# Hybrid encoder layer on Trainium2: where the FFN's first blocks take their weights, and in which order they multiply

## The chip, the cores and the metric

The program runs on one core of one Trainium2 chip. Its engines are TensorE (PE, matrix products), VectorE (DVE), ScalarE (ACT), GpSimd (POOL), and SyncE (SP), which here only issues DMAs. The metric is the device time of one execution in microseconds; the kernel before stands at the median of 3 runs. Where the trace is quoted, times are microseconds from the start of the profiled execution's span, and L12 is line 12 of the kernel that ran.

## The reference, cut to what matters

A layer has three sub-layers with residual adds: token mixing (a gated delta rule beside a spatial gating branch), cross-attention into 256 memory tokens, and a dense SwiGLU FFN. It is computed for two inputs with shared weights: a prompt of 1024 tokens and a sample of 256, D_MODEL 1024, D_FF 2816, all in float32. The change lies where the second sub-layer ends and the third begins:

```python
def rmsnorm(x, w):
    xf = x.astype(jnp.float32)
    y = xf * lax.rsqrt(jnp.mean(xf * xf, -1, keepdims=True) + EPS)
    return (y * w.astype(jnp.float32)).astype(x.dtype)

def encoder_layer(x, mem, ...):
    ...
    x = x + memory_cross_attention(rmsnorm(x, norm_xa_w), rmsnorm(mem, norm_mem_w), xa_w_q, xa_w_kv, xa_w_o)
    h = rmsnorm(x, norm_ffn_w)
    gu = h @ ffn_w_gate_up
    x = x + (jax.nn.silu(gu[..., :D_FF]) * gu[..., D_FF:]) @ ffn_w_down
    return x
```

## The kernel before, in words

Tokens lie in three blocks (b): prompt tokens 0 to 511 (b=0), 512 to 1023 (b=1) and the sample (b=2, 256 columns). A tile x0, x1 or x2 holds one block, features on partitions, in 8 pieces k of 128 features.

A product in float32 precision is three passes: each operand is split into hi (a rounded copy that ACT makes) and lo (the rest, a subtraction on DVE or POOL). `split` (L126 and the line above it) does this; `mm3` issues hi·hi, lo·hi and hi·lo for each 128-row piece, all on line L108. So a "product" below of a 512-column block with 4 pieces is 12 matmuls.

`OutProj.run` (L1227) makes the last projection of the attention, block by block, product m by product m, adds it to x (`evac`, L1237) and collects the squares for the norm: ACT squares (nsq, L248), DVE adds (nacc, L249). `Norm.rest` finishes a norm as a side stream: four or two small matmuls sum nacc over partitions, DVE makes the rsqrt in eleven small operations (L224 to L228, the result is nst), more small matmuls spread nst over the partitions ("the nst matmuls"), DVE scales x (L284) and the pieces are split. Side streams are fed between the matmuls of the main stream by a counted clock of planned matmul time; LAGS and LAGS2 (L2047) are the planned delays in the sample's norm, ahead of the summing matmuls and of the nst matmuls.

The FFN's way up is written with combined operands, which save products: with the two halves of the prompt and of the features, the sinks make differences of the normalised blocks (r1 into block 1's h tiles, L1427; r2 in PSUM banks, L1431; t3, L1538; t4, L1547), each split into hi and lo, and POOL makes sums of gate and up weights. For each f of 22 pieces of D_FF there are four weight pairs: gu_w[f,0] is the gate, [f,1] and [f,2] are sums (`gu_sa`, `gu_sb`), [f,3] is up. w(i) below is gu_w[f,i].

`ff_first` issues f=0 for the prompt and the first two products of f=1 (pn, pn2); `ff_up(1)` starts with the sample's f=0 and f=1 (sg0, su0, sg, su), which need the sample's norm to be done, and ends with f=1's rest; f≥2 is one steady pattern. PE runs matmuls in the order in which the code issues them: before, from the end of the projection, b21·w(0), b11·w(0), r1·w(1), r2·w(1), b22·w(2), then pn, pn2 with gu_w[1,0], then t3·w(2), t4·w(3), the nst matmuls, sg0, su0, sg, and f=1's r2, r1, t3, su, t4, b22. The order on the other engines is a scheduler's, from the code's data flow and estimated times. A queue runs its operations in order.

Before the change, the splits of w(2), w(3) of f=0 and of the gate of f=1 are on DVE (the lines of `split(..., V)` and `gu_gate(1, V)`), and f=1's raw weights are loaded inside ff_first (L1724, L1741). r2 and t3 have tiles of their own in a pool "comb"; sums are made in a tile "room" that is taken when x0 is free.

Of the kernel before, what the change touches and what calls it, by code (L numbers as in the profile page):

```python
# [17 lines left out]
P = 128  # L18
# [145 lines left out]
def trunk_kernel(ctx: ExitStack, tc: tile.TileContext, a):  # L164
# [1040 lines left out]
    class OutProj:  # L1205
# [18 lines left out]
            for m, b in FIRST_PS:  # L1224
                yield from self.parts(m, b, range(KT - 2))

        def run(self, xsrc, scale, wcol, xpool, store, sinks=None, then=None, ready=None):  # L1227

            ps = (xpool,) * 3 if sinks is None else (x0p, xhp, xpool)
            x = [p.tile([P, KT, n], F32, tag=f"x{b}", name=f"x{b}") for b, (p, (_, n)) in enumerate(zip(ps, BLOCKS))]  # L1230
            for ks in (slice(0, 2), slice(2, 8)):
                for b, (t0, n) in enumerate(BLOCKS):
                    SY.dma_start(x[b][:, ks, :], xsrc[:, ks, t0 : t0 + n])
            nms = [Norm(xpool, n) for _, n in BLOCKS]

            def evac(m, b, ps):
                V.scalar_tensor_tensor(out=x[b][:, m, :], in0=ps, scalar=scale, in1=x[b][:, m, :], op0=ALU.mult, op1=ALU.add)  # L1237
# [230 lines left out]
    def gu_sa(f):  # L1468
# [7 lines left out]
        G.tensor_tensor(out=s[:, :512], in0=s[:, 512:], in1=g[:, :512], op=ALU.add)  # L1476
# [15 lines left out]

    def first_weights():
# [23 lines left out]
    ts = ExitStack()  # L1517
    tpool = ts.enter_context(pool("comb"))
# [5 lines left out]
    r2, t3 = ([tpool.tile([P, 4, 512], F32R, tag=f"{name}{i}", name=f"{name}{i}") for i in "hl"] for name in ("r2", "t3"))  # L1524
    gu_w[0, 2], gu_w[0, 3] = pair_of(tpool), pair_of(tpool)

    def parts(hl, k, src, eng):
        split(hl[0][:, k, :], hl[1][:, k, :], src, eng)

    for k in range(4):  # L1530
        parts(r2, k, r2_raw[k], V)
    split(*gu_w[0, 2], gu_raw[0][0], V)
    fs = ExitStack()
    t4 = []

# [6 lines left out]
    def make_t4():  # L1542
        nonlocal fp
        fp = fs.enter_context(pool("ffn", side="right"))
        t4.extend(fp.tile([P, 4, 512], F32R, tag=f"t4{i}", name=f"t4{i}") for i in "hl")
        for k in range(4):
# [3 lines left out]
    def make_room():  # L1550
        nonlocal room
        room = x0p.tile([P, KT, 512], F32, tag="x0", name="room")

    fp = room = None

    turns = {"s": 0, "p": 0}

    def sum_room():
# [8 lines left out]
        S.activation(t, ps, AF.Copy)  # L1567
        return t

    def gu_mm(ps, w, i, x, start):  # L1570

        yield from mm3(ps, [(*wk(w, 4 * i + k), x[0][:, k, :], x[1][:, k, :]) for k in range(4)], start, True, not start)
# [144 lines left out]
    def ff_first():  # L1717
# [6 lines left out]
        SY.dma_start(raw, a["w_gu"][1])  # L1724
# [12 lines left out]
        t2 = gate_of(pf, u2)  # L1737
        make_t4()
        split(*gu_w[0, 3], gu_raw[0][1], V)
        raw = K.raw()[:, :1024]  # L1740
        SY.dma_start(raw, a["w_gu"][NFF + 1])  # L1741
        gu_raw[1].append(raw)
        make_room()
# [6 lines left out]
        c22 = copied(pa, second_block(0))  # L1750
        V.tensor_tensor(out=c22, in0=c22, in1=pe, op=ALU.add)
        times_up(t2, c22, store2(0), -1.0, c22)
        yield from gu_mm(pa, w(3), 1, t4, False)
        times_up(t1, pa, store1(0), -1.0)
        pending["last"] = 0, t1, c22

    def ff_up(f):
        w = lambda i: gu_w[f, i]
        second, last = f == 1, f == NFF - 1
        sums = lambda: (bank()[:, :NS], bank()[:, :NS])  # L1760
        if second:
            pa, pb = first_out
            p1 = copied(pa)
            t1 = gate_of(pb, p1)
            combine(*pending["last"])
            K.finish(K.pending.pop((id(h3), 2)))
            smp.extend(half(h3[2], i) for i in range(2))
            sg0, su0 = sums()
            yield from sample(sg0, gu_w[0, 0], (0, 1))
            gu_sa(1)  # L1770
            ts0 = silu2(sg0, NS)
            sg, su = sums()
            yield from sample(su0, gu_w[0, 3], (0, 1))
            times_up(ts0, su0, gsd[0], 1.0)
        else:
            pa, pb = bank(pm), bank(pm)
            yield from gu_mm(pa, w(0), 0, b11, True)
            p1 = copied(pa)
            sg, su = sums()
            yield from sample(sg, w(0), (0,))  # L1780
            yield from gu_mm(pb, w(0), 1, b21, True)
            t1 = gate_of(pb, p1)
            combine(*pending["last"])
        gu_sb(f)
        gu_load(f + 1, wp if f % 2 == 0 else x2p)
        yield from sample(sg, w(0), (0, 1) if second else (1,))
        yield from gu_mm(pa, w(1), 0, r2, False)
        u2 = copied(pa)
        gu_up(f)
# [341 lines left out]
```

## Time and profile before

| | us |
|---|---|
| runs (3) | 2257.84, 2257.11, 2254.49 |
| median | 2257.11 |
| profiled execution | 2255.0 |
| its span, first to last instruction | 2253.2 |
| mean granted TensorE clock | 0.993 |

The page counts busy time by engine over the span; the windows do so for a stretch, with the granted clock of TensorE (1.00 is full speed). A row of a timeline has start, duration, engine, line, operation, output<-inputs, and in brackets the idle time before it and who ended it. An operand named bank is in PSUM, all others here are in SBUF. In the waits, each row is a waiting engine and line, the operation it waited for, the total, the count and the longest. The touched stage is 1380 to 1464 of the span; f=2 starts at 1464.

### The profile page before, as it was taken

Reading aid. Unit: us, or ns where it says so; the run is one execution under the profiler, and the core shown is the slowest. Engines: PE = TensorE matmul, PEld = TensorE weight load, DVE = VectorE, ACT = ScalarE, POOL = GpSimd, SP = SyncE. Lnnn points to the kernel's source line nnn. Section 1 sums busy time; section 2 is a strip of 40 time slices with the busy share of each in tenths; the row PEclk is TensorE's granted clock in tenths of the full one; section 3 lists DMA queues with packets and bytes.
Section 4 is the critical chain, followed back from the end, with each engine's and each line's share of the span. In section 5 each row is a group of like instructions: output and inputs, shape, how many; then the busy total and the mean of one; then the engine's idle time right before and its main releaser. Section 6 shows DMA issues by size and latency. Waiting matters only on the chain.

```text
span 2253.2 us, 32407 instructions
## 1 busy us (share of the span) xinstructions
PE 2196.2 (97%) x12468; PEld 1918.3 (85%) x12468; DVE 1394.0 (62%) x2770; ACT 815.5 (36%) x1481; POOL 532.7 (24%) x355
## 2 busy tenths in 40 slices
PE   6999999999999999999999999899999999999998
PEld 6988888888888898888888888688888888888888
DVE  7768788887985964664534537544334334568575
ACT  5434243433424433233343423323232323243453
POOL 3010000000000000013231331565666566300031
PEclk9999999999999999999999999999999999999999
DMA  5221322223234445962231431223222222493531
GB/s 185 83 79 68 104 69 87 77 69 95 73 111 125 159 140 165 305 236 94 84 106 45 157 143 57 75 76 110 87 82 76 88 76 82 136 363 126 198 111 57
DMA packets 191301, 262.47 MB, mean 116 GB/s; under 512 B 72410, under 2 KB 102698, under 8 KB 191146
## 3 DMA queue, kind: packets, MB, share of 16 engines
q1 hardware_dynamic: 171306, 231.30, 30.9%
q10 hardware_dynamic: 19840, 29.11, 3.5%
q8 instruction: 97, 1.59, 0.3%
q14 instruction: 58, 0.48, 0.1%
HBM read 182.19 MB, written 78.16 MB: 116 GB/s over the span
## 4 chain that ended last, share of the span: by engine, by line
PE 82%; DVE 8%; issue 4%; DMA 2%; ACT 2%; POOL 1%; SPq 0%; POOLq 0%; ACTq 0%; DVEq 0%
PE bank L108 81%; PE bank L121 1%; DMA tbd<-stage 1%; DVE acc L599 1%; DVE wlo L126 1%; DMA t<-sgd 1%; DVE nt L284 1%; DVE U L845 0%; DVE sw L903 0%; DVE lo L126 0%; DMA stage<-gtd 0%; DVE W L745 0%; DVE nacc L249 0%; DVE aT L714 0%; DVE zt L837 0%
## 5 line engine op out<-in xcount | busy, mean ns | idle before, releaser
L108 PE MATMUL bank<-hi,whi 128*128 128x512 f32 (+1 forms) x2144 | 763.3, 356 | 2.8 <-ACT whi L125 1.7
L108 PE MATMUL bank<-lo,whi 128*128 128x512 f32 (+1 forms) x2144 | 748.8, 349 | 1.1 <-POOL lo L126 1.1
L108 PE MATMUL bank<-hi,wlo 128*128 128x512 f32 (+1 forms) x2144 | 748.3, 349 | 0.9 <-DVE wlo L126 0.9
L108 PEld LDWEIGHTS bank<-hi,wlo 128*128 128x128 f32 x2144 | 406.0, 189 | 54.9 <-DVE wlo L126 1.3
L108 PEld LDWEIGHTS bank<-hi,whi 128*128 128x128 f32 x2144 | 406.9, 190 | 52.7 <-ACT whi L125 2.2
L108 PEld LDWEIGHTS bank<-lo,whi 128*128 128x128 f32 x2144 | 407.1, 190 | 49.8 <-POOL lo L126 1.4
L126 POOL TENSOR_TENSOR wlo<-raw,whi 128x1024 fp32r<-128x1024 f32 x70 | 177.8, 2542 | 377.2 <-ACT whi L125 377.2
L125 ACT ACTIVATE whi<-raw 128x1024 fp32r<-128x1024 f32 (+1 forms) x141 | 144.5, 1026 | 195.3 <-PE bank L108 146.9
L126 POOL TENSOR_TENSOR wlo<-room,whi 128x1024 fp32r<-128x1024 f32 x42 | 100.6, 2396 | 115.7 <-ACT whi L125 115.7
L108 PE MATMUL bank<-bhl,whi 128*128 128x512 f32 x408 | 125.7, 389 | 0.0
L126 DVE TENSOR_TENSOR wlo<-raw,whi 128x1024 fp32r<-128x1024 f32 (+1 forms) x71 | 82.3, 1159 | 43.6 <-ACT whi L125 41.5
L125 ACT ACTIVATE whi<-room 128x1024 fp32r<-128x1024 f32 x42 | 44.6, 1061 | 142.5 <-PE bank L108 138.6
L1796 DVE TENSOR_TENSOR room<-room,bank 128x512 f32<-128x512 f32 x21 | 14.5, 688 | 131.8 <-ACT room L1567 131.8
L108 PEld LDWEIGHTS bank<-bhl,whi 128*128 128x128 f32 x408 | 76.5, 188 | 15.9
L599 DVE SCALAR_TENSOR_TENSOR acc<-craw,sm,acc 128x510 f32<-128x510 f32 (+1 forms) x96 | 73.6, 766 | 20.5 <-ACT acc L597 19.0
L108 PE MATMUL bank<-bhl,wlo 128*128 128x512 f32 x204 | 79.5, 390 | 1.2 <-DVE wlo L126 1.2
L745 DVE TENSOR_TENSOR W<-W,UT 128x2 f32<-128x2 f32 (+30 forms) x155 | 73.2, 472 | 10.1 <-DMA W<-in_eye 5.8
L248 ACT ACTIVATE nsq<-x 128x512 f32<-128x512 f32 (+1 forms) x70 | 40.2, 583 | 102.7 <-DVE x L1237 92.4
L962 ACT ACTIVATE gs<-bank 128x512 f32<-128x512 f32 (+1 forms) x60 | 31.2, 520 | 125.2 <-PE bank L108 119.9
L1589 DVE SCALAR_TENSOR_TENSOR t<-bank,t 128x512 f32<-128x512 f32 (+1 forms) x44 | 24.6, 558 | 82.2 <-PE bank L108 82.2
L249 DVE TENSOR_TENSOR nacc<-nacc,nsq 128x512 f32<-128x512 f32 (+1 forms) x72 | 54.4, 755 | 33.2 <-ACT nsq L248 31.9
L108 PE MATMUL bank<-bhl,ahl 128*128 128x512 f32 x312 | 73.8, 392 | 0.0
(345 smaller groups left out, 4223.1 us busy)
## 6 DMA issues: line engine op xcount, KB each, us to landing
raw<-in_w_gu SPq DMA_DIRECT2D x44, 512.0 KB, 3.9
braw<-gq SPq DMA_DIRECT2D x14, 1024.0 KB, 5.4
raw<-in_w_g SPq DMA_DIRECT2D x20, 512.0 KB, 3.3
gq<-t SPq DMA_DIRECT2D x33, 256.0 KB, 2.0
gtd<-gs ACTq DMA_DIRECT2D x32, 256.0 KB, 2.0
w<-in_w_dn SPq DMA_DIRECT2D x8, 1024.0 KB, 11.9
raw<-in_w_qkv SPq DMA_DIRECT2D x12, 512.0 KB, 3.6
gq<-r SPq DMA_DIRECT2D x22, 256.0 KB, 4.3
```

Of the source, the lines that this page charges most:

```text
L108: self.nc.tensor.matmul(out, l, r, start=start, stop=stop, skip_group_check=more)
L121: self.nc.tensor.transpose(out, x, ident)
L125: self.nc.scalar.activation(hi, src, AF.Copy)
L126: (eng or self.nc.vector).tensor_tensor(out=lo, in0=src, in1=f32(hi), op=ALU.subtract)
L248: S.activation(sq, x, AF.Square)
L249: (eng or V).tensor_tensor(out=self.acc, in0=self.acc, in1=sq, op=ALU.add)
L284: V.scalar_tensor_tensor(out=t, in0=xk(k), scalar=sm[:, wcol + k : wcol + k + 1], in1=pb[:, :n], op0=ALU.mult, op1=ALU.mult)
L599: V.scalar_tensor_tensor(out=dst, in0=src, scalar=wj, in1=dst, op0=ALU.mult, op1=ALU.add)
L745: V.tensor_tensor(out=t3, in0=u3[:, i:, c:].rearrange("p j c -> p c j"), in1=XL[:, 32 * i + i : 32 * i + 32].unsqueeze(1).to_broadcast([P, ...
L962: S.activation(t, ps, AF.Tanh, scale=0.5)
L1589: V.scalar_tensor_tensor(out=out, in0=u, scalar=sign, in1=t, op0=ALU.mult, op1=ALU.mult)
L1796: V.tensor_tensor(out=c22, in0=c22, in1=pe, op=ALU.add)
```

## The change

It alters four things around the end of the projection and the start of the FFN.

- Weights: w(2) and w(3) of f=0 are split by POOL, in the sample's block of the projection, after products m=2 and m=3 (a new hook `after` in `OutProj.run`), into places of the projection's weight pool (now "comb", 6 places of whi and wlo). r2 and t3 live in the other places of that pool. The same two pairs serve as gu_w[f,2] and gu_w[f,3] of all later f (in f=1, [1,1] takes the place of [0,2] and [1,2] gets a pair of wp). The gate of f=1 is split by POOL.
- Loads: f=1's raw weights are loaded after m=3.
- Sums: `room` is x0 itself, so a sum may be written once the part of x0 has been read.
- Order of products: after b22·w(2) comes t3·w(2), then pn, pn2, then t4·w(3), whose four pieces run in the order 2, 3, 0, 1; f=1's r2 and r1 products come before the sample's sg0 and su0. f=1 has a function of its own, `second_up`. LAGS is 20500 instead of 19000 and LAGS2 4000 instead of 8000: the nst matmuls now stand ahead of t4, the summing matmuls after the third matmul of pn.

The diff, cut:

```diff
@@ OutProj.run
+                    if b == 2 and after is not None:
+                        after(m)
@@ sinks
                 split(hi[:, k, :], lo[:, k, :], t, V)
+                if k == KT - 1:
+                    r2_ready()
@@ gu_sa, gu_sb, gu_up
-        hi, lo = gu_w[f, 1] = pair_of(wp)
+        hi, lo = gu_w[f, 1] = gu_w[0, 2] if f == 1 else pair_of(wp)
-        gu_w[f, 2] = pair_of(tpool)
+        gu_w[f, 2] = pair_of(wp) if f == 1 else gu_w[0, 2]
-        gu_w[f, 3] = pair_of(tpool)
+        gu_w[f, 3] = gu_w[0, 3]
@@
-    with pool("wx2", 6) as wx2:
-        K.wx = wx2
-        K.main(op.run(x1d, 1.0, S_FFN, x2p, x2d, sinks, first_weights, copies_read))
+    tpool = ts.enter_context(pool("comb", 6))
+    K.wx = tpool
+    r2, t3 = ((Two(), Two()) for _ in range(2))
+    def after(m):
+        if m == 2:
+            gu_w[0, 2] = room_of()
+            split(*gu_w[0, 2], gu_raw[0][0], G)
+        elif m == 3:
+            gu_w[0, 3] = room_of()
+            split(*gu_w[0, 3], gu_raw[0][1], G)
+            gu_load(1, wp)
+        else:
+            for x, t in zip(r2 if m < 6 else t3, room_of()):
+                x.parts.append(t.rearrange("p (k t) -> p k t", t=512))
+    K.main(op.run(x1d, 1.0, S_FFN, x2p, x2d, sinks, first_weights, copies_read, after))
-    split(*gu_w[0, 2], gu_raw[0][0], V)
+    LAST_FIRST = (2, 3, 0, 1)
+    room = x0
@@ ff_first
-        raw = K.raw()[:, :1024]
-        SY.dma_start(raw, a["w_gu"][1])
-        gu_raw[1] = [raw]
+        make_t3()
         yield from gu_mm(pa, w(1), 0, r2, False)
-        gu_gate(1, V)
-        make_t3()
+        gu_gate(1)
         yield from gu_mm(pf, w(2), 1, b22, True)
...
-        split(*gu_w[0, 3], gu_raw[0][1], V)
+        yield from gu_mm(pa, w(2), 0, t3, False)
+        gu_sa(1)
...
         yield from gu_mm(pn2, gu_w[1, 0], 1, b21, True)
-        yield from gu_mm(pa, w(2), 0, t3, False)
-        yield from gu_mm(pa, w(3), 1, t4, False)
+        yield from gu_mm(pa, w(3), 1, t4, False, LAST_FIRST)
@@ second_up (new, for f=1)
+        combine(*pending["last"])
+        yield from gu_mm(pa, w(1), 0, r2, False)
+        u2 = copied(pa)
+        yield from gu_mm(pe, w(1), 1, r1, True)
+        K.finish(K.pending.pop((id(h3), 2)))
+        yield from sample(sg0, gu_w[0, 0], (0, 1))
+        gu_sb(1)
+        yield from sample(su0, gu_w[0, 3], (0, 1))
+        gu_up(1)
+        gu_load(2, x2p)
+        yield from sample(sg, w(0), (0, 1))
+        gu_gate(2)
+        yield from gu_mm(pa, w(2), 0, t3, False)
+        yield from sample(su, w(3), (0, 1))
+        yield from gu_mm(pa, w(3), 1, t4, False)
+        yield from gu_mm(pe, w(2), 1, b22, False)
+        gu_sa(2)
@@
-LAGS, LAGS2, FIRST_W = 19000, 8000, 9000
+LAGS, LAGS2, FIRST_W = 20500, 4000, 9000
```

What this does to the engines' queues, at three places. The number ahead of a row is its place in the queue; xN at the end are rows alike.

**ACT in the sample's block of the projection** (x_12579 is the sample's x2, x_12577 block 0's, x_12578 block 1's; whi<-raw are the copies of w(2) and w(3) of f=0). Before:

```order
808 L248 ACTIVATE nsq<-x_12578 128x512 x5
809 L248 ACTIVATE nsq<-x_12579 128x256 x2
810 L125 ACTIVATE hi_12891<-x_12577 128x512 x2
811 L248 ACTIVATE nsq<-x_12579 128x256 x2
812 L125 ACTIVATE hi_12891<-x_12577 128x512 x2
813 L125 ACTIVATE hi_12891<-x_12578 128x512
814 L248 ACTIVATE nsq<-x_12579 128x256
815 L125 ACTIVATE whi<-raw 128x1024
```

and now:

```order
808 L248 ACTIVATE nsq<-x_12578 128x512 x5
809 L125 ACTIVATE whi<-raw 128x1024
810 L248 ACTIVATE nsq<-x_12579 128x256
811 L125 ACTIVATE whi<-raw 128x1024
812 L248 ACTIVATE nsq<-x_12579 128x256
813 L125 ACTIVATE hi_12891<-x_12577 128x512 x2
```

The two weight copies moved ahead of the first two squares of the sample.

**POOL from the last split of block 0 on** (lo_12890 are block 0's, lo_13580 and lo_13571 the sample's lo parts; x_12577 as an output is the room for sums). Before:

```order
81 L126 TENSOR_TENSOR lo_12890<-x_12577,hi_12889 128x512 x4
82 L1475 TENSOR_TENSOR room<-raw 128x512
83 L1485 TENSOR_TENSOR room<-raw 128x512
84 L1476 TENSOR_TENSOR room<-room,raw 128x512
85 L1486 TENSOR_TENSOR room<-room,raw 128x512
86 L126 TENSOR_TENSOR wlo<-room,whi 128x1024
87 L126 TENSOR_TENSOR lo_13580<-x_12579,hi_12893 128x256 x4
88 L126 TENSOR_TENSOR wlo<-room,whi 128x1024
89 L126 TENSOR_TENSOR wlo<-raw,whi 128x1024
```

and now:

```order
81 L126 TENSOR_TENSOR lo_12890<-x_12577,hi_12889 128x512 x4
82 L126 TENSOR_TENSOR wlo<-raw,whi 128x1024 x2
83 L1490 TENSOR_TENSOR x_12577<-raw 128x512
84 L1480 TENSOR_TENSOR x_12577<-raw 128x512
85 L1481 TENSOR_TENSOR x_12577<-x_12577,raw 128x512
86 L1491 TENSOR_TENSOR x_12577<-x_12577,raw 128x512
87 L126 TENSOR_TENSOR wlo<-raw,whi 128x1024
88 L126 TENSOR_TENSOR wlo<-x_12577,whi 128x1024
89 L126 TENSOR_TENSOR lo_13571<-x_12579,hi_12893 128x256 x4
90 L1480 TENSOR_TENSOR x_12577<-raw 128x512
91 L1481 TENSOR_TENSOR x_12577<-x_12577,raw 128x512
```

Two weight splits (rows 82) and the split of f=1's gate (87) are new on POOL, the four sums of f=1 stand between them, and the split of the sum (88) is ahead of the sample's lo parts as before; f=2's sums follow at 90.

**DVE from the split of r2 on** (r2l and, now, wlo<-bank are r2's lo parts; t3l and wlo<-x_12578 t3's). Before:

```order
1791 L126 TENSOR_TENSOR r2l<-bank,r2h 128x512 x4
1792 L126 TENSOR_TENSOR wlo<-raw,whi 128x1024
1793 L1584 TENSOR_TENSOR copies<-copies,bank 128x512
1794 L1538 TENSOR_TENSOR x_12578<-x_12578 128x512 x2
1795 L1580 SCALAR_TENSOR_TENSOR t<-t,copies 128x512
1796 L126 TENSOR_TENSOR t3l<-x_12578,t3h 128x512 x2
1797 L1538 TENSOR_TENSOR x_12578<-x_12578 128x512 x2
1798 L126 TENSOR_TENSOR wlo<-raw,whi 128x1024
1799 L126 TENSOR_TENSOR t3l<-x_12578,t3h 128x512 x2
```

and now:

```order
1791 L126 TENSOR_TENSOR wlo<-bank,whi 128x512 x4
1792 L1612 TENSOR_TENSOR copies<-copies,bank 128x512
1793 L1568 TENSOR_TENSOR x_12578<-x_12578 128x512 x3
1794 L1608 SCALAR_TENSOR_TENSOR t<-t,copies 128x512
1795 L126 TENSOR_TENSOR wlo<-x_12578,whi 128x512 x3
1796 L1568 TENSOR_TENSOR x_12578<-x_12578 128x512
1797 L1761 TENSOR_TENSOR copies<-copies,bank 128x512
1798 L1577 SCALAR_TENSOR_TENSOR x_12577<-bank,x_12577 128x512
1799 L126 TENSOR_TENSOR wlo<-x_12578,whi 128x512
```

The weight splits are gone from DVE, and three of t3's differences now stand ahead of its first split.

More of the change, by code (lines that the diff above doesn't have):

```diff
@@ L1225, in begin, with run @@
                 yield from self.parts(m, b, range(KT - 2))
-        def run(self, xsrc, scale, wcol, xpool, store, sinks=None, then=None, ready=None):
+        def run(self, xsrc, scale, wcol, xpool, store, sinks=None, then=None, ready=None, after=None):
             ps = (xpool,) * 3 if sinks is None else (x0p, xhp, xpool)
@@ L1511, in first_weights, with __init__, __getitem__, room_of @@
         K.side(sums())
-    with pool("wx2", 6) as wx2:
-        K.wx = wx2
-        K.main(op.run(x1d, 1.0, S_FFN, x2p, x2d, sinks, first_weights, copies_read))
+    class Two:
+        def __init__(self):
+            self.parts = []
+        def __getitem__(self, key):
+            return self.parts[key[1] // 2][key[0], key[1] % 2, key[2]]
+    ts = ExitStack()
+    tpool = ts.enter_context(pool("comb", 6))
+    K.wx = tpool
+    r2, t3 = ((Two(), Two()) for _ in range(2))
+    def room_of():
+        return tuple(tpool.tile([P, 1024], F32R, tag=t, name=t) for t in ("whi", "wlo"))
+    def after(m):
[9 more added lines that the diff above has]
+                x.parts.append(t.rearrange("p (k t) -> p k t", t=512))
+    def parts(hl, k, src, eng):
+        split(hl[0][:, k, :], hl[1][:, k, :], src, eng)
+    def r2_ready():
+        for k in range(4):
+            parts(r2, k, r2_raw[k], V)
+    K.main(op.run(x1d, 1.0, S_FFN, x2p, x2d, sinks, first_weights, copies_read, after))
     x0, x1 = op.x[0], op.x[1]
-    ts = ExitStack()
-    tpool = ts.enter_context(pool("comb"))
     K.finish(K.pending.pop((id(h3), 1)))
@@ L1523, in trunk_kernel @@
     first_copies = hp.tile([P, 4, 512], F32, tag="lo2", name="copies")
[L1524 to L1531, printed above, removed]
-    split(*gu_w[0, 2], gu_raw[0][0], V)
     fs = ExitStack()
@@ L1545, in make_t4 @@
         t4.extend(fp.tile([P, 4, 512], F32R, tag=f"t4{i}", name=f"t4{i}") for i in "hl")
-        for k in range(4):
+        for k in LAST_FIRST:
             V.scalar_tensor_tensor(out=x0[:, k + 4, :], in0=r2_raw[k], scalar=-1.0, in1=x0[:, k + 4, :], op0=ALU.mult, op1=ALU.subtract)
             parts(t4, k, x0[:, k + 4, :], V)
[L1550 to L1554, printed above, removed]
+    fp = None
+    LAST_FIRST = (2, 3, 0, 1)
+    room = x0
     turns = {"s": 0, "p": 0}
@@ L1568, in copied, with gu_mm @@
         return t
-    def gu_mm(ps, w, i, x, start):
-        yield from mm3(ps, [(*wk(w, 4 * i + k), x[0][:, k, :], x[1][:, k, :]) for k in range(4)], start, True, not start)
+    def gu_mm(ps, w, i, x, start, ks=range(4)):
+        yield from mm3(ps, [(*wk(w, 4 * i + k), x[0][:, k, :], x[1][:, k, :]) for k in ks], start, True, not start)
     def ff(p, tag, name, n=512, bufs=None):
@@ L1738, in ff_first @@
         make_t4()
-        split(*gu_w[0, 3], gu_raw[0][1], V)
[L1740 to L1743, printed above, removed]
+        yield from gu_mm(pa, w(2), 0, t3, False)
+        gu_sa(1)
+        c22 = copied(pa, second_block(0))
+        V.tensor_tensor(out=c22, in0=c22, in1=pe, op=ALU.add)
+        times_up(t2, c22, store2(0), -1.0, c22)
         pn = bank(pm)
@@ L1757, in ff_up @@
     def ff_up(f):
         w = lambda i: gu_w[f, i]
-        second, last = f == 1, f == NFF - 1
+        last = f == NFF - 1
         sums = lambda: (bank()[:, :NS], bank()[:, :NS])
[L1761 to L1783, printed above, removed]
+        pa, pb = bank(pm), bank(pm)
@@ L1784, in ff_up @@
+        yield from gu_mm(pa, w(0), 0, b11, True)
+        p1 = copied(pa)
+        sg, su = sums()
+        yield from sample(sg, w(0), (0,))
+        yield from gu_mm(pb, w(0), 1, b21, True)
+        t1 = gate_of(pb, p1)
+        combine(*pending["last"])
         gu_sb(f)
         gu_load(f + 1, wp if f % 2 == 0 else x2p)
-        yield from sample(sg, w(0), (0, 1) if second else (1,))
+        yield from sample(sg, w(0), (1,))
         yield from gu_mm(pa, w(1), 0, r2, False)
@@ L1816, in up @@
         yield from ff_first()
-        for f in range(1, NFF):
+        yield from second_up()
+        for f in range(2, NFF):
             yield from ff_up(f)
```

23 lines of the change are left out of this document (20 added, 3 removed).

## The prediction

> **What bounds the kernel now.** The page first, then windows of the touched stage and of what follows it (length, busy time of PE, PEld, DVE, ACT and POOL, the granted clock, the DMA's share, GB/s):
>
> ```profile
> PE 2196.2 (97%) x12468; PEld 1918.3 (85%) x12468; DVE 1394.0 (62%) x2770; ACT 815.5 (36%) x1481; POOL 532.7 (24%) x355
> ```
>
> ```profile
> 1390.00:1400.00 10.00, 10.00 (x76) 9.59 (x75) 10.00 (x21) 6.27 (x12) 0.00 (x0) 1.00 0.00 0
> 1400.00:1410.00 10.00, 9.21 (x41) 7.25 (x41) 9.07 (x15) 4.17 (x9) 0.00 (x0) 1.00 0.32 107
> 1410.00:1420.00 10.00, 6.77 (x30) 4.76 (x30) 10.00 (x17) 6.08 (x10) 0.00 (x0) 1.00 0.14 52
> 1420.00:1430.00 10.00, 8.19 (x35) 6.08 (x33) 8.62 (x21) 2.95 (x5) 3.21 (x3) 1.00 0.14 52
> 1430.00:1440.00 10.00, 4.76 (x19) 4.17 (x20) 8.31 (x16) 4.27 (x9) 8.16 (x7) 0.54 0.33 105
> 1470.00:1790.00 320.00, 320.00 (x1694) 276.23 (x1694) 132.03 (x143) 95.23 (x129) 198.60 (x103) 1.00 0.26 89
> ```
>
> PE is the bound nearly everywhere; between 1400 and 1440 it is not. There DVE is full (10.00, 9.07, 10.00) and POOL idle until 1427. The waits of PE between 1380 and 1464 say on whom (total, times, longest):
>
> ```profile
> PE bank L108 <- DVE nst L228: 4.3, 1, 4.3
> PE bank L108 <- ACT whi L125: 1.7, 1, 1.7
> PE bank L108 <- DVE wlo L126: 0.9, 1, 0.9
> ```
>
> The longest is for nst, the rsqrt of the sample's norm, which DVE finishes late; PE's timeline around it, and the start of f=2 (its first hi,whi):
>
> ```profile
> 1428.48 0.40 PE L108 MATMUL bank<-t4h,wlo 128*128 128x512 f32 x1
> 1433.16 1.22 PE L108 MATMUL bank<-cst,nst 128*128 128x128 f32 x4 [4.28 <-DVE nst L228]
> 1435.40 0.58 PE L108 MATMUL bank<-hi,whi 128*128 128x256 f32 x1 [1.02 <-ACT hi L125]
> 1437.05 0.58 PE L108 MATMUL bank<-lo,whi 128*128 128x256 f32 x1 [1.06 <-POOL lo L126]
> 1463.82 0.39 PE L108 MATMUL bank<-hi,wlo 128*128 128x512 f32 x1
> 1464.04 0.39 PE L108 MATMUL bank<-hi,whi 128*128 128x512 f32 x1
> ```
>
> From 1470 to 1790 PE is busy for all of 320 us at full clock, and the change leaves the order of products from f=2 on alone, so it is worth what it moves 1464.04 by. The part after nst adds up: from 1433.16 to 1464.04 are 30.9 us. In them lie 60 matmuls of 512 columns at 0.227 us (1463.82 to 1464.04, the mean of neighbours), 13.6 us; 96 of 256 columns at 0.12, 11.5; the four nst matmuls, some 0.4; together 25.5. The other 5.4 are the two waits for hi and lo (start to start some 1.8 and 1.5) and some 2 us of half clock.
>
> **The lock that the change walks into.** Before, POOL does nothing while DVE is full. Where both run, DVE's operations on two SBUF operands end only after POOL's (POOL's and DVE's timelines):
>
> ```profile
> 1317.73 2.40 POOL L126 TENSOR_TENSOR wlo<-raw,whi 128x1024 fp32r<-128x1024 f32 x1 [0.31 <-ACT whi L125]
> 1318.20 2.48 DVE L249 TENSOR_TENSOR nacc<-nacc,nsq 128x512 f32<-128x512 f32 x1 [0.94 <-ACT nsq L248]
> 1379.73 0.69 DVE L249 TENSOR_TENSOR nacc<-nacc,nsq 128x512 f32<-128x512 f32 x1 [0.76 <-ACT nsq L248]
> 1429.56 1.25 POOL L1476 TENSOR_TENSOR room<-room,raw 128x512 f32<-128x512 f32 x1
> 1429.59 1.78 DVE L1580 SCALAR_TENSOR_TENSOR t<-t,room 128x512 f32<-128x512 f32 x1
> 1462.49 2.40 POOL L126 TENSOR_TENSOR wlo<-room,whi 128x1024 fp32r<-128x1024 f32 x1 [1.72 <-ACT whi L125]
> 1464.24 0.69 DVE L1584 TENSOR_TENSOR room<-room,bank 128x512 f32<-128x512 f32 x1 [2.05 <-PE bank L108]
> ```
>
> nacc takes 0.69 alone and 2.48 beside a split: it ends at 1320.68, 0.55 after POOL. So does L1580 (1431.37 against 1430.81). L1584, with one operand in a bank (PSUM), keeps its 0.69. So I charge a DVE operation on two SBUF tiles that starts while POOL runs with the rest of POOL's operation (for 256 columns ending 0.3 after it). The Trainium skill, page "SBUF — State Buffer", section "SBUF: two separate sides", speaks against the change in the same sense: the port pair of DVE and GpSimd is an exclusive lock for a whole instruction, and a DVE instruction with two SBUF inputs contends for it. By that rule the sum is the same as by the rows, which agree.
>
> **Part by part.** (1) *Splits of w(2) and w(3) go to POOL, and to products m=2 and m=3 of the sample block.* The whi copy can start when PE has read the weights whose place it takes, which is when that product is evacuated:
>
> ```profile
> 1382.45 0.42 DVE L1237 SCALAR_TENSOR_TENSOR x<-bank,x 128x256 f32<-128x256 f32 x1
> 1382.96 0.42 ACT L248 ACTIVATE nsq<-x 128x256 f32<-128x256 f32 x1 [3.26 <-DVE nst L228]
> 1384.34 0.16 DVE L228 SCALAR_TENSOR_TENSOR nst<-bank,nst 128x4 f32<-128x4 f32 x1
> 1387.18 0.43 DVE L249 TENSOR_TENSOR nacc<-nacc,nsq 128x256 f32<-128x256 f32 x1 [0.54 <-ACT nsq L248]
> 1387.52 1.40 DVE L284 SCALAR_TENSOR_TENSOR x<-x,sm,bank 128x512 f32<-128x512 f32 x2
> 1398.78 1.05 ACT L125 ACTIVATE whi<-raw 128x1024 fp32r<-128x1024 f32 x1
> 1406.15 2.48 DVE L126 TENSOR_TENSOR r2l<-bank,r2h 128x512 fp32r<-128x512 f32 x4
> 1406.89 0.50 PE L108 MATMUL bank<-r2l,whi 128*128 128x512 f32 x1 [0.79 <-DVE r2l L126]
> 1408.54 1.22 DVE L126 TENSOR_TENSOR wlo<-raw,whi 128x1024 fp32r<-128x1024 f32 x1
> ```
>
> ACT copies whi at 1382.3 to 1383.35 (1.05, L125); POOL splits 1383.4 to 1385.8 (2.40). ACT's queue now holds nsq behind that whi, so nacc comes at about 1383.7, always inside POOL's operation: it ends near 1386.05. The last links of block 1's rsqrt stand behind it; three at 0.2 us each give nst at 1386.6, not 1384.5, and PE, which has no other work queued before nst, loses **1.9 us**. m=3 repeats it: PE 1.9 late, whi 1388.0, POOL 1389.1 to 1391.5, nacc held until 1391.7, and L284 and all of block 1's normalisation behind it begin at 1391.7 instead of 1387.5: DVE is **4.2 us late**. It is full from there (windows), so the one gap of 0.9 that it had, against one more nacc held by a POOL sum of f=1 near 1402 (1.2), leaves r2l 4.2 late: 1410.35. PE is only 1.9 late when it asks, and idles some **3.3 us** before r2l, at 1411.1.
>
> (2) *DVE from r2l to nst.* In the change's order 29 operations of 512 columns stand in that stretch: 29 by 0.60 (2.48 for four, less the overlap) is 17.4; the rsqrt's 11 small ones at 0.2 are 2.2; a wait for ACT's silu, queued behind gate(1)'s whi, 0.6. Three DVE splits of 1.22 are gone. Three operations meet POOL: t3's first difference a sum of f=1 (0.9), the two silu products the splits of gate(1) and of sa(1) (1.7 each): 4.3. Sum **24.5 us**, from 1410.35 to **1434.85**; before, 27.0 from 1406.15 to 1433.1. PE's work in front of nst is 59 matmuls, 13.4 us, well inside; its waits for gate(1)'s weights (1.7 and 0.9) are replaced by waits for t3 and a final one of some 5 us for nst, 1.8 us later than now.
>
> (3) *From nst to f=2.* t4, r2 and r1 (36 matmuls, 8.2 us) now stand between nst and the sample's products, and hide the split into hi and lo: the 1.8 and 1.5 go. That takes 12 matmuls of t4 behind nst: 72 by 0.227 is 16.3, plus 11.5 and 0.5: 28.3. Half clock as before, 2.0, since PE's gap ahead of nst grows.
>
> SP issues the loads of f=2's pieces when DVE has made the last lo. Before, that was at 1439.7, 6.6 us after nst; now three operations on f=0's results and one held by POOL's lo stand among them, some 2.2 more, so 1443.6. POOL's queue behind that transfer is two sums, a split, two sums and the split that su needs:
>
> ```profile
> 1438.37 1.35 DVE L126 TENSOR_TENSOR lo<-x,hi 128x256 fp32r<-128x256 f32 x2
> 1409.91 0.33 SPq L1724 DMA_DIRECT2D raw<-in_w_gu  x1
> 1423.51 0.33 SPq L1741 DMA_DIRECT2D raw<-in_w_gu  x1
> ```
>
> ```profile
> raw<-in_w_gu SPq DMA_DIRECT2D x44, 512.0 KB, 3.9
> w<-in_w_dn SPq DMA_DIRECT2D x8, 1024.0 KB, 11.9
> ```
>
> Landing at 1448 (3.9 and the second issue's 0.4), then 4 by 1.25 and 2 by 2.4 give 1458: su waits about **1.1 us**. Each further microsecond of landing is one more. f=1's own loads move from 1409.9 and 1423.5 to about 1386 and 1391.5, behind POOL's two splits on SP's queue; what they pass, x2's last store, nobody in this stage waits for. *Sums in x0, shared places:* I cost these at nothing. From f=2 on, w(2)'s one place is read last by b22, the end of a turn, and next by t3; between lie b11, b21, r2, r1 (48 matmuls, 10.9 us) and sg (24, 2.9), which hide the copy and the split (1.05 and 2.40). Without that cover each of 20 turns would pay up to 3.5.
>
> Sum: 1434.85 + 0.1 + 28.3 + 2.0 + 1.1 = 1466.3, **2.3 us later** than 1464.04. Bounds of the held operations: nothing (no row shows a free one beside POOL) to the full 2.40 more each, of which I take the rows' rule. The execution profiled took 2255.0 us (span 2253.2), 2.1 below the median of 2257.11: 2257.3 in its terms, **2259** against the median.
>
> **Rivals.** *No hold bites.* If DVE and POOL miss each other, r2l stays at 1406.15, the stretch is 20.2, nst 1426.4, and f=2 some 30.7 later at 1457.1: 7 us earlier, 2250. For it: DVE's short operations leave POOL gaps. Against: nacc follows whi on ACT, so it meets POOL by construction.
>
> *Only the first two miss.* nst at 1431.0, f=2 at 1462.4, 1.6 earlier: 2255.5. It needs a POOL split that starts 0.4 later than its whi ends; at 1317.73 it started within 0.31 of its cause.
>
> *Slower: the clock stays halved from the gap at r2l.* It fell 2.0 us after the last matmul ended and came back only after unbroken work:
>
> ```profile
> 1430.70:1430.90 0.20, 0.00 (x0) 0.00 (x0) 0.20 (x1) 0.00 (x0) 0.12 (x2) 1.00 0.00 0
> 1430.90:1431.10 0.20, 0.00 (x0) 0.00 (x0) 0.20 (x1) 0.00 (x0) 0.20 (x1) 0.50 0.00 0
> 1441.10:1441.30 0.20, 0.20 (x3) 0.20 (x3) 0.00 (x0) 0.00 (x0) 0.00 (x0) 0.90 1.08 430
> ```
>
> The gaps of 3.3 at r2l and about 3 at t3 are longer than 2.0. If it halves at 1411 and stays, the 59 matmuls take 26.8, nst's matmuls come at 1437.9, 3.0 later, and nearly 1 more of half clock follows: 3.9 over the forecast, 2263. A drop of one stretch costs nothing, for the wait at t3 swallows it; it decides once PE's work, not DVE's, ends last before nst. The Trainium skill, page "TensorE: Matmul & The Clock Gate", Part 1, wants an idle window of about 3.4 us before the clock halves; by it 3.3 us would not do. The trace's 2.0 us speaks otherwise.
>
> *f=2's pieces land late,* as the 1024 KB of w_dn do (11.9): su 8 us later, 2267. 512 KB never has that median.
>
> **How the numbers follow.** Forecast 0.50, no hold 0.13, first two missed 0.12, clock 0.17, late pieces 0.08. The forecast's own range is 2256 to 2262, landing and half clock varying by a few microseconds. The median is known to about 0.2%, 4.5 us: the same means 2252.6 to 2261.6. Faster 0.18 (no hold 0.13, tails of the next 0.05), slower 0.30 (clock 0.16, late 0.08, the forecast's upper tail 0.06), same 0.52. The range 2251 to 2265 leaves out most of the first and last cases.
>
> **What would show it.** DVE's L249 at 256 columns beside POOL's wlo near 1383 and 1389 at 2.3 us, not 0.43; PE waits for nst (1.9 near 1386.6, 5 near 1435) and for r2l (3.1); no waits for hi or lo; PE at half clock after 1430; f=2 near 1466. Wrong if nacc keeps 0.43, or if PE's busy time between 1400 and 1420 grows.

## The result, and the profile after

The changed kernel takes 2259.16 us (median of 15 runs, 2256.51 to 2263.36), the kernel before 2257.30 (15 runs, 2254.49 to 2258.54). The ratio is 1.0012 with a 95% interval of 1.0005 to 1.0019: slower by some 2.7 us (1.1 to 4.3), clear of no change but below 0.2%. The two medians differ by 1.9. The forecast was 2259 us, with 2.3 us more in the touched stage.

The profiled execution took 2260.03 us, 5.0 more than the one before. Half of that is not the change's. DVE's evacuation of block 1's last product, the last thing ahead of the touched stage, starts 2.4 us later than in the profile before, where it started at 1378.28; f=2 starts at 1468.91, where it was 1464.04 (DVE's and PE's timelines of the changed kernel):

```profile
1380.72 0.69 DVE L1238 SCALAR_TENSOR_TENSOR x<-bank,x 128x512 f32<-128x512 f32 x1 [3.30 <-PE bank L108]
1468.91 0.39 PE L108 MATMUL bank<-hi,whi 128*128 128x512 f32 x1
```

So everything below is counted from that evacuation. The **stage**, from it to f=2's first matmul, was 85.76 us and is 88.19: 2.43 longer. From f=2 to the end of the span are 789.2 us before and 789.3 now.

The windows over the stage (length, busy time of PE, PEld, DVE, ACT and POOL, granted clock, the DMA's share, GB/s):

```profile
1380.00:1390.00 10.00, 8.04 (x64) 7.54 (x63) 5.85 (x15) 2.00 (x3) 2.37 (x1) 1.00 0.62 222
1390.00:1400.00 10.00, 10.00 (x73) 10.00 (x73) 8.39 (x13) 2.99 (x6) 2.38 (x1) 0.83 0.26 94
1400.00:1410.00 10.00, 10.00 (x60) 8.89 (x59) 10.00 (x19) 5.49 (x11) 1.95 (x1) 1.00 0.21 69
1410.00:1420.00 10.00, 7.58 (x33) 5.63 (x31) 10.00 (x13) 4.53 (x8) 7.06 (x4) 1.00 0.11 37
1420.00:1430.00 10.00, 8.70 (x33) 7.16 (x34) 9.88 (x15) 5.48 (x9) 2.41 (x1) 0.83 0.16 52
1430.00:1440.00 10.00, 4.95 (x18) 3.84 (x18) 8.28 (x24) 3.26 (x7) 0.85 (x2) 0.75 0.00 0
```

POOL now works while DVE is full, DVE's load is no smaller (busy for 52.4 of the 60 us from 1380 to 1440, where it was 52.2), and PE is idle, at the longest, in three places. The waits of PE in 1380 to 1470:

```profile
PE bank L108 <- DVE nst L228: 6.8, 2, 5.1
PE bank L108 <- ACT copies L1595: 2.9, 1, 2.9
PE bank L108 <- POOL wlo L126: 1.0, 1, 1.0
PE bank L108 <- DVE wlo L126: 0.8, 1, 0.8
```

The waits for gate(1)'s weights, for hi and for lo are gone. In their place stand a second wait for nst (1.8, block 1's norm), one for t3 (2.9, shown as ACT's copy, which is queued behind a late t3h) and one for su's weights (1.0). Their source is in POOL's and DVE's timelines:

```profile
1385.98 2.37 POOL L126 TENSOR_TENSOR wlo<-raw,whi 128x1024 fp32r<-128x1024 f32 x1 [20.20 <-ACT whi L125]
1386.23 2.40 DVE L249 TENSOR_TENSOR nacc<-nacc,nsq 128x256 f32<-128x256 f32 x1 [0.24 <-ACT nsq L248]
1391.78 2.38 POOL L126 TENSOR_TENSOR wlo<-raw,whi 128x1024 fp32r<-128x1024 f32 x1 [3.43 <-ACT whi L125]
1392.04 2.40 DVE L249 TENSOR_TENSOR nacc<-nacc,nsq 128x256 f32<-128x256 f32 x1 [0.89 <-ACT nsq L248]
1415.13 4.90 DVE L1568 TENSOR_TENSOR x<-x 128x512 f32<-128x512 f32 x3
1427.36 2.48 DVE L1608 SCALAR_TENSOR_TENSOR t<-t,copies 128x512 f32<-128x512 f32 x1
```

An operation of DVE that ends only after POOL's is called held below. Additions that took 0.43 take 2.40, ending 0.28 after POOL's operation each time; three differences of 0.6 each take 4.90, one silu product of 0.69 takes 2.48. PE's timeline has the answer to each:

```profile
1389.16 1.16 PE L108 MATMUL bank<-cst,nst 128*128 128x128 f32 x8 [1.79 <-DVE nst L228]
1412.88 0.50 PE L108 MATMUL bank<-wlo,whi 128*128 128x512 f32 x1 [0.79 <-DVE wlo L126]
1421.30 0.80 PE L108 MATMUL bank<-whi 128*128 128x512 f32 x1 [2.92 <-ACT copies L1595]
1436.85 1.19 PE L108 MATMUL bank<-cst,nst 128*128 128x128 f32 x4 [5.05 <-DVE nst L228]
1460.64 0.39 PE L108 MATMUL bank<-hi,wlo 128*128 128x256 f32 x1 [0.96 <-POOL wlo L126]
```

### The profile page after: what moved, and what is told of

Same layout as the page of the kernel before. It is cut to its first block, busy times and chain, and to the rows that moved or that the text cites. A ratio compares the mean times of both kernels' runs of the same rounds, so it can differ in the third digit from the quotient of the medians.

```text
span 2258.2 us, 32409 instructions
## 1 busy us (share of the span) xinstructions
PE 2199.2 (97%) x12468; PEld 1921.0 (85%) x12468; DVE 1401.8 (62%) x2767; ACT 815.3 (36%) x1481; POOL 538.9 (24%) x358
## 5 line engine op out<-in xcount | busy, mean ns | idle before, releaser
L126 POOL TENSOR_TENSOR wlo<-x,whi 128x1024 fp32r<-128x1024 f32 x42 | 100.8, 2401 | 53.2 <-ACT whi L125 53.2
L1842 DVE TENSOR_TENSOR x<-x,bank 128x512 f32<-128x512 f32 x20 | 13.8, 690 | 118.9 <-ACT x L1595 118.9
L1608 DVE SCALAR_TENSOR_TENSOR t<-t,x 128x512 f32<-128x512 f32 x42 | 64.9, 1545 | 29.1 <-ACT t L1607 29.1
L249 DVE TENSOR_TENSOR nacc<-nacc,nsq 128x512 f32<-128x512 f32 (+1 forms) x72 | 59.3, 823 | 32.1 <-ACT nsq L248 30.8
L125 ACT ACTIVATE whi<-x 128x1024 fp32r<-128x1024 f32 (+1 forms) x46 | 47.0, 1023 | 81.5 <-PE bank L108 74.1
L1617 DVE SCALAR_TENSOR_TENSOR t<-bank,t 128x512 f32<-128x512 f32 (+1 forms) x44 | 24.6, 558 | 82.4 <-PE bank L108 82.4
```

The source lines that it names most:

```text
L125: self.nc.scalar.activation(hi, src, AF.Copy)
L126: (eng or self.nc.vector).tensor_tensor(out=lo, in0=src, in1=f32(hi), op=ALU.subtract)
L249: (eng or V).tensor_tensor(out=self.acc, in0=self.acc, in1=sq, op=ALU.add)
L1608: V.scalar_tensor_tensor(out=t, in0=t, scalar=1.0, in1=src, op0=ALU.add, op1=ALU.mult)
L1617: V.scalar_tensor_tensor(out=out, in0=u, scalar=sign, in1=t, op0=ALU.mult, op1=ALU.mult)
```

## The experiments

All start from the changed kernel. This table collects them: the start of the stage, the stage, how long after its start the sample's nst matmuls begin, and the ratio of the whole time to the kernel before, run on the same chip.

| kernel | start | stage | nst matmuls after | ratio to before (95%) |
|---|---|---|---|---|
| before | 1378.28 | 85.76 | 54.88 | |
| changed | 1380.72 | 88.19 | 56.13 | 1.0012 (1.0005 to 1.0019) |
| changed, again | 1378.07 | 87.92 | 56.12 | 1.0009 (1.0000 to 1.0017) |
| squares in PSUM | 1381.12 | 84.62 | 52.51 | 0.9998 (0.9989 to 1.0007) |
| w(2), w(3) split on DVE | 1377.03 | 85.60 | 53.74 | 1.0004 (0.9995 to 1.0013) |
| gate(1) split on DVE | 1376.67 | 86.96 | 54.81 | 0.9999 (0.9990 to 1.0008) |
| squares in PSUM and gate(1) on DVE | 1377.44 | 83.32 | 51.39 | 0.9991 (0.9982 to 0.9999) |
| old splits, new order | 1379.96 | 88.16 | 56.16 | 1.0015 (1.0005 to 1.0024) |
| old delays | 1380.83 | 87.06 | 58.75 | 1.0015 (1.0003 to 1.0027) |
| both repairs, wait filled | 1376.98 | 78.39 | 51.16 | 0.9966 (0.9954 to 0.9979) |
| the same, again | 1377.76 | 77.99 | 51.14 | 0.9968 (0.9957 to 0.9979) |
| both repairs, wait half filled | 1377.14 | 80.33 | 51.12 | 0.9981 (0.9972 to 0.9990) |
| wait filled, no repair | 1380.11 | 84.90 | 57.84 | 0.9993 (0.9984 to 1.0001) |

The column of starts spans 4.4 us, in kernels whose code ahead of the stage is the same, while from f=2 to the end of the span all of them take 788.8 to 789.6: as far as the profiled executions show, that is what blurs the ratios, and the stage is free of it. Each stage is read from one execution; the two kernels that were profiled twice differ by 0.3 and 0.4 in it.

**Squares in PSUM.** It takes the hold away and leaves POOL's work where it is: ACT writes the two squares to a bank, so that DVE's addition has one operand in PSUM. The edit, cut:

```diff
-                sq = self.p.tile([P, 512], F32, tag="nsq", name="nsq", bufs=3)[:, : self.n]
+                sq = (bank() if ps else self.p.tile([P, 512], F32, tag="nsq", name="nsq", bufs=3))[:, : self.n]
@@ evac
-                nms[b].add(x[b][:, m, :])
+                nms[b].add(x[b][:, m, :], ps=after is not None and b == 2 and m in (2, 3))
```

> The changed kernel, but the sample's squares of products m=2 and m=3 are written to PSUM banks, so DVE's two nacc additions there have one PSUM operand; POOL's splits stay where they are. The stage is counted from the start of DVE's evacuation of block 1's last product (512 columns) to f=2's first matmul: 85.8 us before, 88.2 in the changed kernel. Theory (DVE's operation on two SBUF tiles is held by POOL's): the two additions take 0.4 to 0.5 us instead of 2.40, PE's 1.8 us before block 1's nst matmuls is gone, r2l comes about 3.5 us earlier, the stage is 84.0 and the time 4 us below the changed kernel (2255). Rival (the additions are late because of ACT's order, or the product order costs the 2.4): they still end with POOL's split, stage 88, time unchanged within 1 us.

The stage is 84.62, 3.6 shorter, and the ratio falls from 1.0012 to 0.9998. DVE's and POOL's timelines of this kernel:

```profile
1386.38 2.37 POOL L126 TENSOR_TENSOR wlo<-raw,whi 128x1024 fp32r<-128x1024 f32 x1 [20.20 <-ACT whi L125]
1386.60 0.42 DVE L249 TENSOR_TENSOR nacc<-nacc,bank 128x256 f32<-128x256 f32 x1 [0.21 <-ACT bank L248]
1390.23 2.41 POOL L126 TENSOR_TENSOR wlo<-raw,whi 128x1024 fp32r<-128x1024 f32 x1 [1.50 <-ACT whi L125]
1390.47 0.42 DVE L249 TENSOR_TENSOR nacc<-nacc,bank 128x256 f32<-128x256 f32 x1 [0.87 <-ACT bank L248]
```

Same place, same POOL operation 0.2 us ahead, 0.42 instead of 2.40. Nothing but the second operand's home changed, so the hold is shown, and with it 3.6 us. The rival that ACT's order or the product order costs falls for this part.

**w(2) and w(3) split on DVE**, at the same places: `split(*gu_w[0, 2], gu_raw[0][0], V)` and the like for w(3).

> The changed kernel with the lo parts of w(2) and w(3) made by DVE instead of POOL, at the same places. Theory: two operations of 1.22 us on DVE replace two holds of about 2: PE waits about 1 us before block 1's nst matmuls, nst of the sample comes about 2 us earlier, stage 86.0, time 2 us below the changed kernel. Rival (moving the work off DVE is worth what DVE's busy time shows, and something else costs): DVE gets 2.4 us more work, stage 90 or more, slower by 2.

The stage is 85.60, 2.6 shorter although DVE has 2.4 us more work: handing 1.2 us to POOL costs DVE 2 where it can be held. The two holds stand in a chain: PE's wait ahead of block 1's nst matmuls is 0.92 instead of 1.79, and block 1's normalisation (L284) starts 11.27 after the start of the stage instead of 13.64.

**gate(1) split on DVE**: `gu_gate(1, V)`.

> The changed kernel with the lo part of f=1's gate made by DVE (1.22 us) instead of POOL. Theory: the hold of 3 us on t3's differences near 1417 goes, DVE gains some 1.2 net, stage 87.0, time 1 us below the changed kernel. Rival: DVE is only given 1.22 more, stage 89.4, 1 us slower.

The stage is 86.96, 1.2 shorter. The three differences now take 2.73 instead of 4.90, and the hold by sa(1)'s split has moved on to a split of t4:

```profile
1411.04 2.73 DVE L1568 TENSOR_TENSOR x<-x 128x512 f32<-128x512 f32 x3
1420.83 2.44 DVE L126 TENSOR_TENSOR t4l<-x,t4h 128x512 fp32r<-128x512 f32 x1
```

**Both.** Squares in PSUM and gate(1) on DVE.

> Squares of m=2 and m=3 in PSUM and f=1's gate split on DVE, otherwise the changed kernel. Theory: the gains add, stage 83.1, time 5 us below the changed kernel and 3 below the kernel before (2254). Rival: within 1 us of the changed kernel.

The stage is 83.32: the gains of 3.6 and 1.2 add. This kernel is 2.4 us shorter in the stage than the one before, with nst's matmuls at 51.39 instead of 54.88. PE's longest wait is still for nst (its timeline):

```profile
1428.83 0.55 PE L108 MATMUL bank<-cst,nst 128*128 128x128 f32 x1 [6.20 <-DVE nst L228]
```

**Old splits, new order.** w(2) and w(3) are split by DVE after r2, as before the change. The edit, cut:

```diff
     def after(m):
         if m == 2:
             gu_w[0, 2] = room_of()
-            split(*gu_w[0, 2], gu_raw[0][0], G)
         elif m == 3:
             gu_w[0, 3] = room_of()
-            split(*gu_w[0, 3], gu_raw[0][1], G)
-            gu_load(1, wp)
@@ r2_ready
             parts(r2, k, r2_raw[k], V)
+        split(*gu_w[0, 2], gu_raw[0][0], V)
+        split(*gu_w[0, 3], gu_raw[0][1], V)
+        gu_load(1, wp)
```

> The changed kernel, but w(2) and w(3) of f=0 are split by DVE after r2, as in the kernel before, and f=1's loads follow there; the places, the sums and the new order of products stay, and f=1's gate stays on POOL. Theory (DVE's row of work up to nst ends last, whatever PE's order): block 1's wait for nst and the late r2l are gone, DVE has two splits of 1.22 more ahead of nst, so nst comes where it came before give or take 1 us and the stage is about 87, 1 us shorter than in the changed kernel and still not shorter than before. Rival (the new order of products is good by itself, the holds ate its gain): the stage is 82 to 83.

The stage is 88.16, not 87: block 1's wait and the late r2l are gone, but nst is at 56.16, as in the changed kernel. The two splits stand ahead of t3, and POOL's work now holds DVE's operations there: gate(1)'s split and a sum of f=1 hold two splits of t3 for 2.6 us, and sa(1)'s split the second silu product for 2.0 (POOL's and DVE's timelines):

```profile
1416.12 3.49 POOL L126 TENSOR_TENSOR wlo<-raw,whi 128x1024 fp32r<-128x1024 f32 x1 [51.12 <-DMA raw<-in_w_gu]
1419.56 1.72 POOL L1480 TENSOR_TENSOR x<-raw 128x512 f32<-128x512 f32 x1
1425.56 2.41 POOL L126 TENSOR_TENSOR wlo<-x,whi 128x1024 fp32r<-128x1024 f32 x1
1417.90 3.94 DVE L126 TENSOR_TENSOR wlo<-x,whi 128x512 fp32r<-128x512 f32 x2
1425.87 2.65 DVE L1608 SCALAR_TENSOR_TENSOR t<-t,copies 128x512 f32<-128x512 f32 x1 [1.64 <-ACT t L1607]
```

The rival's 82 to 83 did not come. But this kernel does not show what the new order is worth by itself, since 4.6 us of holds are still in it; the old splits in the new order with no hold at all were not run.

**Old delays.** LAGS 19000 and LAGS2 8000.

> The changed kernel with the planned delays of the kernel before (19000 and 8000 instead of 20500 and 4000): the summing matmuls of the sample's norm come earlier and the nst matmuls behind t4. Theory: nst is no sooner, for DVE's queue decides; stage 88.5, within 1 us of the changed kernel, with t4 done before the wait and a shorter wait for nst (3.5 instead of 5). Rival (the nst matmuls' place is what costs): 2 us or more either way.

The stage is 87.06, 1.1 shorter, just outside what was expected. nst's matmuls are at 58.75, behind t4, with 3.4 us of wait, so nst itself came 2.6 us later than in the changed kernel; the expectation gives no reason for that. In this execution t3·w(2), with the summing matmuls among its own, ran at half clock for longer (granted clock 0.57 between 1420 and 1428, where the changed kernel has 0.79). ACT's copy for sa(1), behind it, comes 46.85 after the start of the stage instead of 45.03, and the silu product 48.46 instead of 46.64. How much of this the delays cause, and how much the clock, is not separated. What is left after nst's matmuls is 28.3 us: 60 matmuls of 512 columns (13.6), 96 of 256 (11.5), 0.4, a wait of 2.3 for su's weights, together 27.8. No half clock follows the gap of 3.41 here (a window of this kernel behind its nst matmuls):

```profile
1439.00:1446.00 7.00, 6.42 (x32) 5.48 (x33) 5.55 (x15) 3.68 (x9) 3.12 (x4) 1.00 0.20 75
```

while the changed kernel pays it (a window of that one):

```profile
1437.40:1441.00 3.60, 3.60 (x12) 2.92 (x11) 2.92 (x8) 2.01 (x5) 1.56 (x2) 0.50 0.00 0
```

Its whole time is no better (1.0015), and the interval does not settle 1 us.

**Wait filled.** With both repairs nst is still fixed by DVE and PE waits 6.2 us for it. f=1's r2 and r1 need nothing from the sample, so they were moved ahead of t4, and nst's matmuls behind them; t4's pieces run in another order. The edit without the two repairs, cut:

```diff
@@ ff_first, behind pn2
+        p1 = copied(pn)
+        early[1] = gate_of(pn2, p1)
+        yield from gu_mm(pn, gu_w[1, 1], 0, r2, False)
+        early[2] = copied(pn)
+        early[3] = bank(pm)
+        yield from gu_mm(early[3], gu_w[1, 1], 1, r1, True)
         yield from gu_mm(pa, w(3), 1, t4, False, LAST_FIRST)
@@ second_up
-        p1 = copied(pa)
-        t1 = gate_of(pb, p1)
+        t1, u2, pe = early[1], early[2], early[3]
         combine(*pending["last"])
-        yield from gu_mm(pa, w(1), 0, r2, False)
-        u2 = copied(pa)
-        pe = bank(pm)
-        yield from gu_mm(pe, w(1), 1, r1, True)
@@
-    LAST_FIRST = (2, 3, 0, 1)
+    LAST_FIRST = (2, 1, 3, 0)
-LAGS, LAGS2, FIRST_W = 20500, 4000, 9000
+LAGS, LAGS2, FIRST_W = 20500, 9000, 9000
```

> Experiment with both repairs (squares in PSUM, gate split on DVE), and f=1's products r2 and r1 moved ahead of t4 (t4's pieces in the order 2, 1, 3, 0), with the nst matmuls behind them (LAGS2 9000). Theory (nst is fixed by DVE, so PE should have the 24 matmuls that it can already do in front of it): the wait of 6 us for nst falls under 1, no half clock after it, stage 78.6, 4.7 us shorter than with the repairs alone, time about 7 below the kernel before (2248). Rival (a later wait takes it back: hi and lo of the sample, or the weights behind f=2's loads): stage 82 or more.

The stage is 78.39, 7.4 us shorter than before the change; 2246.75 us (median of 5 runs) against 2254.61 for the kernel before on the same chip, 0.9966 (0.9954 to 0.9979). PE's waits of this kernel:

```profile
PE bank L108 <- ACT x L1595: 2.1, 1, 2.1
PE bank L108 <- DVE wlo L126: 1.4, 2, 0.8
PE bank L108 <- ACT copies L1595: 0.8, 1, 0.8
PE bank L108 <- POOL lo L126: 0.4, 1, 0.4
PE bank L108 <- ACT hi L125: 0.3, 1, 0.3
PE bank L108 <- DVE nst L228: 0.3, 1, 0.3
```

nst's share fell from 6.2 to 0.3; what it covered of hi and lo comes back as 0.7, and f=1's t4 waits 2.1 for ACT's copy, which is queued behind the whi copy of a sum that POOL finishes late. The clock stays at 1.00 from 1390 to 1440; with the repairs alone it is 0.50 between 1428 and 1432.

> As the run before with LAGS2 6500: the nst matmuls stand between r2 and r1. Theory: wait for nst about 3 us, but r1 then covers the split of the sample, stage 78.5, equal within 0.5. Rival: the wait for nst is longer by 2.7 and nothing covers, stage 81.

With LAGS2 6500 the stage is 80.33, 1.8 above the expectation and nearer to the rival's 81. The wait for nst is 2.97 as expected, and r1 covers hi and lo, for which PE no longer waits. But the wait brings a stretch at half clock, which the expectation left out: the granted clock is 0.73 between 1431 and 1434, and from 1429.28 to 1432.67 eight matmuls start 0.42 apart instead of 0.23, which costs 1.6 (a window and PE's timeline):

```profile
1431.00:1434.00 3.00, 3.00 (x11) 2.44 (x10) 2.85 (x8) 1.71 (x5) 2.13 (x3) 0.73 0.00 0
1429.28 0.63 PE L108 MATMUL bank<-hi,wlo 128*128 128x512 f32 x1
1432.67 0.39 PE L108 MATMUL bank<-lo,whi 128*128 128x512 f32 x1
```

> The changed kernel with f=1's products r2 and r1 moved ahead of t4 and the nst matmuls behind them (LAGS2 9000, t4's pieces 2, 1, 3, 0), without the two repairs. Theory (two things cost in the changed kernel, DVE's holds and PE's wait for nst with work at hand): the holds stay, 2.4 us each on the two nacc additions, r2l and t3 are as late as in the changed kernel, but no wait for nst; stage 84.6, 3.6 us shorter than the changed kernel and 1.2 than the one before. Rival (the holds alone explain the changed kernel, PE's order is free): stage 88.

The moved products without the repairs: stage 84.90, 3.3 shorter than the changed kernel. So the changed kernel loses to both, the holds and the wait, and mending either alone puts its stage ahead of the kernel before (83.32 and 84.90 against 85.76). In this run PE does not wait for the sample's nst: its own work ends last, with the clock at 0.57 between 1420 and 1428.

The changed kernel and the filled one once more, on one chip:

> The changed kernel once more, beside the other two on the same chip. Stage 88.2 within 0.5; the time of the whole program may differ by some 2 us from the profile of before, since the start of the stage lies between 1376.7 and 1381.1 in the runs so far with no difference of code ahead of it.

> The kernel with both repairs and the moved products once more, beside the changed kernel. Stage 78.4 within 0.5, 9.8 us shorter than the changed kernel's; time 7 to 8 us below the kernel before and 10 below the changed one, if what lies outside the stage is equal.

The stages are 87.92 and 77.99; the ratios 1.0009 and 0.9968 differ by 9.3 us, where the stages differ by 9.9.

## Why the prediction was right, point by point

**The hold.** Right, and shown: the two additions at 2.40 as charged (2.3), and at 0.42 once an operand is in PSUM. The rivals without a hold, or without the first two, did not come.

**Block 1's nst.** 1.9 forecast, 1.79 measured. **r2l** was to be 4.2 late; on the stage's clock it is at 1412.14 less 1380.72, 31.42, where it was 27.87 (1406.15 less 1378.28): 3.6 late. The term that was mis-sized is the third hold, 1.2 us on an addition near 1402. POOL's sum started 0.38 before that addition, and still the addition took 0.42; it was POOL's sum that took longer, 1.95 instead of 1.29:

```profile
1404.99 1.95 POOL L1490 TENSOR_TENSOR x<-raw 128x512 f32<-128x512 f32 x1 [10.83 <-DVE bank L1434]
1405.37 0.42 DVE L249 TENSOR_TENSOR nacc<-nacc,nsq 128x256 f32<-128x256 f32 x1
```

So the prediction's rule, that a DVE operation on two SBUF tiles is charged when it starts while POOL runs, does not hold for every row. PE's gap ahead of r2l was forecast twice, as 3.3 and as 3.1; the terms (0.79, 4.2 more, 1.9 less) give 3.1. It was 0.79, after a stretch at half clock, and 2.24 in the changed kernel's second profile, where there was none.

**From r2l to nst.** 24.5 us forecast; from 1412.14 to the end of the last nst operation (1436.71) it is 24.6. The sum held, its parts not quite: the three differences are held for 3.1 us, by a sum and by gate(1)'s split one after the other, and the silu product that was to wait for gate(1) is free. 2.6 was charged to the two. sa(1)'s split held the second silu product for 1.8, as forecast (1.7).

**From nst's matmuls to f=2.** Forecast 31.4 (28.3, 2.0 of half clock, 1.1 for su): 1468.91 less 1436.85 is 32.1. These 0.7 more and the 0.6 by which r2l came sooner than forecast cancel, so that the sum is right to 0.1 us is in part luck. su waited 0.96, so the rival of late pieces for f=2 did not come either. The cover of hi and lo worked.

**The clock.** The forecast kept one drop, after nst. In the profile there were three: after the 1.79 us gap at block 1's nst already, after t3's, and after the sample's nst. That the first costs nothing, because the wait behind it shrinks, can be read from the changed kernel's two profiles: with the clock at 0.83 between 1390 and 1400, PE waits 0.79 for r2l; in the second, at 1.00 there, it waits 2.24, 1.45 more, and the stage is 0.3 shorter (second profile, window and PE's timeline; the gap at block 1's nst is the same 1.79):

```profile
1390.00:1400.00 10.00, 10.00 (x83) 9.91 (x82) 10.00 (x17) 2.59 (x5) 1.53 (x1) 1.00 0.16 52
```

```profile
1386.51 1.16 PE L108 MATMUL bank<-cst,nst 128*128 128x128 f32 x8 [1.79 <-DVE nst L228]
1410.18 0.50 PE L108 MATMUL bank<-wlo,whi 128*128 128x512 f32 x1 [2.24 <-DVE wlo L126]
```

The rival in which PE's work ends last before nst, because the clock stays halved, did not come: 0.83 and 0.83 over 10 us are 3.4 us at half each, and PE still waits 5.05 for nst. One of the signs of being wrong did come in the first profile: PE is busy for 17.58 us between 1400 and 1420, where it was 15.98. In the second it is 14.84. The first profile's stage starts 2.4 us later, so read at these times the sign decides nothing. On the threshold the Trainium skill, page "TensorE: Matmul & The Clock Gate", Part 1, asks for an idle window of about 3.4 us before the clock halves; here a gap of 1.79 us was followed by half clock once and not the other time, so the measurement decides against that threshold; 3.4 us is the length of the two short stretches at half clock.

**The total.** +2.3 in the stage against +2.43 and +2.2; the level of 2259 rests on adding the 2.1 us by which the profile before lay under its median, and came out at 2259.16, with the median before at 2257.30 where the forecast had 2257.11.

What stays open: why the start of the stage scatters by 4.4 us, which is more than the change's whole effect, and what decided between the two executions whether the clock fell at the first gap; neither was tried. What the new order of products is worth without any hold is not shown either.

## What to carry to other kernels

Before work goes from a full DVE to an idle POOL, look at which DVE operations will run beside it: one that reads two SBUF tiles and starts behind POOL's mostly ends only after it, so that 1.2 us of split handed over cost 2 us here, and where the order of a third engine ties the two together (here ACT's copy ahead of the square) they met in both profiles of the changed kernel. With one operand in PSUM the addition kept its 0.42. And where PE waits for a chain that another engine fixes, reordering what stands behind the wait gains only what it covers; first find products that can be moved ahead of it: 24 matmuls moved, with both repairs in place, took 4.9 us off the stage.

## What the runs showed of the hardware that was not expected

Half clock can follow a gap of PE of 1.79 us (changed kernel, 0.83 between 1390 and 1400), and the same gap can pass without it (second profile, 1.00). Longer gaps passed too: 2.9 us ahead of t3 with w(2) and w(3) split on DVE (1.00 between 1410 and 1424), and 3.41 us ahead of nst with the old delays (1.00 between 1439 and 1446). And the hold works both ways: POOL's sum near 1405 took 1.95 instead of 1.29 beside DVE's operations, and gate(1)'s split took 2.89 instead of 2.40 between two of t3's differences:

```profile
1414.81 1.30 POOL L1491 TENSOR_TENSOR x<-x,raw 128x512 f32<-128x512 f32 x1
1416.60 2.89 POOL L126 TENSOR_TENSOR wlo<-raw,whi 128x1024 fp32r<-128x1024 f32 x1 [0.50 <-ACT whi L125]
```
